# Four moves of work between engines in a one-core hybrid decoder layer

## The chip, the cores and the metric

The kernel runs on one core of one Trainium2 chip. The metric is the device time of one execution in microseconds (us), first instruction to last as the device reports it; lower is better. The engines are TensorE (PE in the rows; PEld is its weight load), VectorE (DVE), ScalarE (ACT), GpSimd (POOL) and SyncE (SP, which here issues nearly all the transfers). Each engine runs its own instructions strictly in the order in which they were written down for it.

## What is computed

One decoder layer for one sequence: SEQ = D_MODEL = 1024, all in float32. Cut to what matters here:

```python
mod = jnp.dot(jax.nn.silu(c), w_ada) + b_ada          # adaLN, 6 vectors of 1024
shift1, scale1, gate1, shift2, scale2, gate2 = split(mod, 6)
h = _rmsnorm(x, norm1_w) * (1.0 + scale1) + shift1
qa, ka, va, iq, ik, iw, qr, kr, vr, gr, ga, gb = split(jnp.dot(h, w_in))
# qa, ka, iq, ik, qr, kr are rotated by their positions
score = einsum('bqh,bqhs->bqs', iw, relu(einsum('bqhd,bsd->bqhs', iq, ik)))   # indexer
idx   = top_k(score, 256)                              # per query, causal
y_a   = attention(qa, ka, va, over idx only) @ w_attn_proj
ret   = retention(qr, kr, vr)                          # 4 heads, chunks of 128
y_r   = (silu(gr) * groupnorm_per_head(ret)) @ w_ret_proj
x = x + gate1 * ((sigmoid(ga) * y_a + sigmoid(gb) * y_r) @ w_out)
h2 = _rmsnorm(x, norm2_w) * (1.0 + scale2) + shift2
x = x + gate2 * ((silu(h2 @ w_gate) * (h2 @ w_up)) @ w_down)
return _rmsnorm(x, final_norm_w)
```

## The kernel before, in words

Every matrix product is done as three passes of 32-bit matmuls over a split of both factors in a high and a low part (`whi`, `wlo`, `hT_hi`, `hT_lo`). The high part is a copy on ACT, the low part a subtraction on POOL (L80, L756) or on DVE; the pairs live in a ring of 11. The weights come in by SP as blocks of 128x512 or 128x1024.

The order of the work on each engine is fixed ahead of time by a scheduler that goes through the program with priorities. `turns_after(a, b)` adds an order (no wait of its own): `a` is placed behind `b` in the list of instructions. Work whose priority is lowered by `LATE` fills places that the scheduler deems free. The stages, with the times at which the profiled execution is there:

- Startup, to about 100 us: the norm of x, the modulation vectors shift1 and scale1, and the first projections.
- V projection and indexer scores, about 100 to 230 us. `score_units` (L403) works out the score tiles; between them stand the first of 32 *modulation steps* of `mod_work` (L506). They are for the four vectors that are needed later: first m = 2 and 5 (the gates), then m = 3 and 4 (shift2, scale2). A step loads a block `mw` of 128x1024 of `w_ada` (two buffers) and adds it, times a column of silu(c), to `macc` on DVE (L525 for a vector's first step, L527 for the other seven). Behind the eighth step of a gate, `mod_gate` (L554) multiplies `macc` by a tile of ones on PE and adds the vector's bias, which `gateb` has from a broadcast load (one buffer, one load and one sum on L562 per half). Behind the eighth step of m = 3 and 4, `mod_cols` (L541) transposes `macc` (L547) and reduces it (L548, L550, L552). Each step is tied behind `summed[-1]`, the last score sum that was written down.
- The search, `select_all` (L449): the 256th largest score of each row is found by bisection, bit by bit. One pass is six counts `eq` (L463, tiles of 128x384 to 128x1024) and two small instructions (`rej` L468, `cand` L483), all on DVE; there are 31 passes and a last one. The passes have low priority, and some are tied to points of the program by the list `passes`.
- Retention, about 230 to 474 us: for two pairs of heads (`hp` = 0, 1) a *qk stage* (project, rotate, transpose) and a *V stage*. In the V stage each of eight tiles projects `vs`, makes two scores `inn` (`inner`: PE L674, DVE L676) and runs a chunk of the tile before for two heads (`chunk`: PE L684, L685, L689; DVE `rst` L693/L695; ACT `on` L698; DVE statistics L701 and L702, of which the last is kept in `chunked[0]`). In the V stage of `hp` = 0 two modulation steps are written down behind each tile.
- The gate stage, about 474 to 840 us: products with the weights of gr, q, k, gb and ga, in `Stream` objects that save one product in eight by sums of blocks (seven products `M1` to `M7` of 12 matmuls each). The results gather in `kept`, `sums` and `spare`, where `add` (L824, DVE) adds a product and `copy` (L821, ACT) starts one. `behind(i)` (L1029) runs behind product i: it ties search passes to `genv.added` and rotates the first channels of q and k, which earlier streams put in `rot_d`. `rope_load` fetches one half of the tokens, `rope_store` multiplies it by the tables (POOL L991, L992, L994, L995), adds (DVE L993, L996), splits (ACT L755, POOL L756) and stores.
- Attention, projections, FFN and the last norm, 840 us to the end.

## Time and profile before

| | |
|---|---|
| runs | 1747.34 us median of 3 (1744.49 to 1750.73) |
| profiled execution | 1744.53 us, its span 1742.7 us |
| mean granted TensorE clock | 0.995 |
| busy: PE, DVE, ACT, POOL | 97%, 71%, 43%, 49% of the span |

The profiled execution ran on one core and its trace holds every instruction with its start, its duration and, where its engine sat idle ahead of it, what released it. The span runs from the first instruction to the last; the execution's own time is 1.8 us longer. A share of busy time is a mean over stages that have different limits. What a change is worth is found where PE, the engine with 97%, sits idle: there a row says how long and which instruction ended it.

### The profile page before, as it was taken

What the parts mean: (1) busy time and instruction counts of PE and PEld (TensorE: products, weight loads), DVE (VectorE), ACT (ScalarE), POOL (GpSimd) and SP (SyncE); (2) the same over time, 40 slices, a digit from 0 to 9 for tenths busy, and PEclk for the clock granted to TensorE, in tenths of its full rate; (3) what the DMA queues carried; (4) which work ended last, traced back from release to release, by engine and by line L of the source; (5) the groups of instructions that cost most, each with busy time, mean ns of one, the idle gap of its engine ahead of it and who ended that gap; (6) DMA issues with size and microseconds to landing.
All of it is one profiled execution on the core that took longest, in us unless ns stands there. A gap on an engine that the chain in (4) does not pass through costs nothing.

```text
span 1742.7 us, 24594 instructions
## 1 busy us (share of the span) xinstructions
PE 1685.4 (97%) x8266; PEld 1391.7 (80%) x8266; DVE 1234.4 (71%) x2118; ACT 755.3 (43%) x1469; POOL 856.8 (49%) x855
## 2 busy tenths in 40 slices
PE   5899999999999999999999999999999999999998
PEld 4797777888887887888777888888888888878887
DVE  7528798898899577666576666885666555778664
ACT  3625542332454344530477235643333333445444
POOL 4563274583615578130346550055455554657573
PEclk9999999999999999999999999999999999999999
DMA  9535515412434356865761740044445444586652
GB/s 293 151 95 176 152 55 173 143 34 60 117 98 127 108 151 200 252 205 165 186 142 53 274 169 1 25 133 148 157 134 180 173 146 144 187 305 205 197 169 97
DMA packets 180063, 260.72 MB, mean 150 GB/s; under 512 B 13584, under 2 KB 111328, under 8 KB 177632
## 3 DMA queue, kind: packets, MB, share of 16 engines
q1 hardware_dynamic: 179936, 259.14, 47.6%
q8 instruction: 65, 1.06, 0.3%
q14 instruction: 62, 0.51, 0.1%
HBM read 192.51 MB, written 66.58 MB: 149 GB/s over the span
## 4 chain that ended last, share of the span: by engine, by line
PE 64%; DVE 3%; issue 1%; DMA 1%; POOL 1%; ACT 1%; SPq 0%; POOLq 0%; DVEq 0%; ACTq 0%
PE ya L843 4%; PE ya L841 4%; PE ya L845 4%; PE yb L843 3%; PE yb L841 3%; PE yb L845 3%; PE ya L1664 2%; PE ya L1663 2%; PE ya L1662 2%; PE pva L1183 2%; PE mm L841 2%; PE mm L843 2%; PE mm L845 2%; PE tra L1162 2%; PE lg L841 1%; PE lg L843 1%
## 5 line engine op out<-in xcount | busy, mean ns | idle before, releaser
L80 POOL TENSOR_TENSOR wlo<-wraw,whi 128x512 fp32r<-128x512 f32 (+2 forms) x116 | 147.9, 1285 | 136.6 <-ACT whi L77 100.1
L463 DVE TENSOR_SCALAR_CACHE_REDUCE eq<-score,cand 128x384 uint8<-128x384 f32 (+2 forms) x192 | 180.7, 941 | 4.0
L756 POOL TENSOR_TENSOR flo<-tmp,fhi 128x512 fp32r<-128x512 f32 x79 | 108.2, 1369 | 140.1 <-ACT fhi L755 100.5
L121 PE MATMUL mm<-whi,hT_hi 128*128 128x512 f32 (+1 forms) x432 | 162.0, 380 | 4.0 <-ACT qk L647 1.8
L123 PE MATMUL mm<-wlo,hT_hi 128*128 128x512 f32 (+1 forms) x432 | 161.6, 377 | 0.0
L124 PE MATMUL mm<-whi,hT_lo 128*128 128x512 f32 (+1 forms) x432 | 161.5, 376 | 0.0
L841 PE MATMUL ya<-hc,fhi 128*128 128x512 f32 x344 | 133.9, 390 | 2.0 <-DVE c L824 2.0
L843 PE MATMUL ya<-hc,fhi 128*128 128x512 f32 x344 | 134.1, 390 | 0.6 <-DVE hc L1302 0.6
L845 PE MATMUL ya<-hc,flo 128*128 128x512 f32 x344 | 133.1, 390 | 0.0
L1641 ACT ACTIVATE dslot<-draw 128x512 fp32r<-128x512 f32 x143 | 84.9, 627 | 93.1 <-DMA draw<-act_d 23.2
L756 POOL TENSOR_TENSOR flo<-raws,fhi 128x512 fp32r<-128x512 f32 x60 | 86.3, 1445 | 73.8 <-ACT fhi L755 42.4
L1642 DVE TENSOR_TENSOR dslot<-draw,dslot 128x512 fp32r<-128x512 f32 x81 | 86.4, 1098 | 50.7 <-ACT dslot L1641 49.3
L1642 POOL TENSOR_TENSOR dslot<-draw,dslot 128x512 fp32r<-128x512 f32 x62 | 95.5, 1554 | 53.0 <-ACT dslot L1641 51.0
L77 ACT ACTIVATE whi<-wraw 128x512 fp32r<-128x512 f32 (+2 forms) x116 | 67.2, 591 | 117.3 <-DMA wraw<-in_w_in_dram 56.6
L755 ACT ACTIVATE fhi<-tmp 128x512 fp32r<-128x512 f32 x82 | 51.5, 629 | 111.5 <-PE ya L843 57.2
L843 PE MATMUL yb<-hc,fhi 128*128 128x512 f32 x256 | 99.7, 390 | 0.0
L841 PE MATMUL yb<-hc,fhi 128*128 128x512 f32 x256 | 99.7, 389 | 0.0
L845 PE MATMUL yb<-hc,flo 128*128 128x512 f32 x256 | 99.5, 389 | 0.0
L121 PEld LDWEIGHTS mm<-whi,hT_hi 128*128 128x128 f32 x432 | 81.5, 190 | 16.1 <-ACT qk L647 2.2
L809 DVE TENSOR_TENSOR tmp<-raws 128x512 f32<-128x512 f32 x40 | 30.6, 768 | 86.7 <-POOL flo L756 86.7
L124 PEld LDWEIGHTS mm<-whi,hT_lo 128*128 128x128 f32 x432 | 81.7, 189 | 12.4
L1151 POOL TENSOR_SCALAR sx<-sx,mx 128x128 f32<-128x128 f32 (+7 forms) x64 | 47.4, 747 | 88.9 <-DVE mx L1150 66.3
(419 smaller groups left out, 4959.6 us busy)
## 6 DMA issues: line engine op xcount, KB each, us to landing
draw<-act_d SPq DMA_DIRECT2D x70, 256.0 KB
mw<-in_w_ada_dram SPq DMA_DIRECT2D x32, 512.0 KB
act_d<-c SPq DMA_DIRECT2D x58, 256.0 KB
raw<-in_w_in_dram SPq DMA_DIRECT2D x26, 512.0 KB
raws<-in_w_ffn_gate_dram SPq DMA_DIRECT2D x24, 512.0 KB
raws<-in_w_ffn_up_dram SPq DMA_DIRECT2D x24, 512.0 KB
dw<-in_w_ffn_down_dram SPq DMA_DIRECT2D x22, 512.0 KB
dw_d<-dw SPq DMA_DIRECT2D x10, 1024.0 KB
```

What stands on the lines that cost most here:

```text
L77: ins = nc.scalar.activation(hi[:, :n], raw[:, :n], AF.Copy)
L80: nc.gpsimd.tensor_sub(lo[:, :n], raw[:, :n], f32(hi[:, :n]))
L121: ins = nc.tensor.matmul(ps, lhsT=ahi, rhs=whi[:, :n], start=(i == 0), stop=False)
L123: nc.tensor.matmul(ps, lhsT=ahi, rhs=wlo[:, :n], start=False, stop=False)
L124: nc.tensor.matmul(ps, lhsT=alo, rhs=whi[:, :n], start=False, stop=(i == last))
L463: ins = [nc.vector.tensor_scalar(eq[:, :sc.shape[1]], sc, thr[j], None, op0=op, op1=ALU.add, accum_out=cnt[:, j:j + 1]) for j, sc in enume ...
L756: return ins, (eng or nc.gpsimd).tensor_sub(lo, src, f32(hi))
L841: mm = nc.tensor.matmul(ps, lhsT=whi[:, k, :], rhs=hhi[:, k, :], start=own and k == 0, stop=False, skip_group_check=True)
L843: nc.tensor.matmul(ps, lhsT=whi[:, k, :], rhs=hlo[:, k, :], start=False, stop=False, skip_group_check=True)
L845: nc.tensor.matmul(ps, lhsT=wlo[:, k, :], rhs=hhi[:, k, :], start=False, stop=k == 3, skip_group_check=True)
L1641: nc.scalar.activation(slot[:, 0], raw, AF.Copy)
L1642: lo_eng.tensor_sub(slot[:, 1], raw, f32(slot[:, 0]))
```

## The change

It has four parts.

1. The bias row of a gate comes by one load of 128x1024, written down at the fourth step of its vector, in place of two loads of 128x512 in `mod_gate`. The tile of ones moves into `spare`, to make room.
2. In the V stage of `hp` = 0 the modulation steps from the second tile on are tied behind the statistics of the tile (`chunked[0]`), where they were tied behind the last score sum.
3. The search passes that are tied to the gate stage's groups are each tied two groups later: pass 22 stands where pass 24 did, and so on.
4. `rope_store` becomes a generator of three steps, one step behind each of six products: the four multiplications on POOL, the sum and difference on DVE, and the split with its stores. The second half is loaded at M6 in place of M7.

```diff
@@ -500,7 +500,7 @@
-    ones = modp.tile([P, P], F32, name="ones")
+    ones = spare[:, :P]
     nc.vector.memset(ones, 1.0)
@@ -527,10 +527,12 @@
             if behind is not None:
                 turns_after(ins, behind)
+            if k == 3 and m in (2, 5):
+                bias = gate_bias(m)
             yield
             if k == KT - 1:
                 if m in (2, 5):
-                    mod_gate(m, m // 5, acc)
+                    mod_gate(m // 5, acc, bias)
@@ -551,12 +553,15 @@
-    def mod_gate(m, i, acc):
+    def gate_bias(m):
+        bias = modp.tile([P, D], F32, name="gateb", bufs=1)
+        nc.sync.dma_start(out=bias, in_=b_ada[m * D:(m + 1) * D].rearrange("(o d) -> o d", o=1).partition_broadcast(P))
+        return bias
+
+    def mod_gate(i, acc, bias):
         for hf in range(2):
             cs = slice(hf * H, (hf + 1) * H)
-            g = modp.tile([P, H], F32, name="gateb", bufs=1)
-            nc.sync.dma_start(out=g, in_=b_ada[m * D + hf * H:m * D + (hf + 1) * H]
-                              .rearrange("(o d) -> o d", o=1).partition_broadcast(P))
+            g = bias[:, cs]
             gp = ps_lg()
@@ -722,6 +727,8 @@
             if hp == 0:
+                if t:
+                    summed.append(chunked[0])
                 for _ in range(2):
                     next(mgen, None)
@@ -985,15 +992,18 @@
-    def rope_store(hf, r, tab):
+    def rope_turn(hf, r, tab):
+
         cs = slice(hf * H, (hf + 1) * H)
         t = [f32(x) for x in ring_pair()]
         nc.gpsimd.tensor_mul(t[0], r[0], tab[0])
         nc.gpsimd.tensor_mul(t[1], r[1], tab[1])
-        nc.vector.tensor_sub(t[0], t[0], t[1])
         nc.gpsimd.tensor_mul(r[0], r[0], tab[1])
         nc.gpsimd.tensor_mul(r[1], r[1], tab[0])
+        yield
+        nc.vector.tensor_sub(t[0], t[0], t[1])
         nc.vector.tensor_add(r[1], r[1], r[0])
+        yield
         for a, src in enumerate((t[0], r[1])):
@@ -1024,22 +1034,22 @@
-    rope, staged = {}, {}
+    rope, staged = [], {}
...
-        if i >= 15 and (i - 15) % 7 == 0 and 24 + (i - 15) // 7 < len(passes) - 1:
-            turns_after(passes[24 + (i - 15) // 7], genv.added)
+        if i >= 15 and (i - 15) % 7 == 0 and 22 + (i - 15) // 7 < len(passes) - 1:
+            turns_after(passes[22 + (i - 15) // 7], genv.added)
...
-            if n == 8 and m in ("M1", "M7"):
-                rope[len(rope)] = rope_load(len(rope))
-            if n == 9 and m in ("M5", "M2"):
-                rope_store(int(m == "M2"), *rope[int(m == "M2")])
+            if n == 8 and m in ("M1", "M6"):
+                rope.append(rope_turn(len(rope), *rope_load(len(rope))))
+            if n == 9 and m != "M4":
+                next(rope[int(m in ("M3", "M7", "M2"))], None)
```

How the instructions stand on an engine is listed below for three places, before and with the change (`out<-in` and the shape; line numbers are those of the kernel listed, so L676 before is L681 with the change). First DVE at the first score `inn` of the V stage of `hp` = 0. Before:

```order
L463 TENSOR_SCALAR eq,cnt<-score_769,cand 128x512
L463 TENSOR_SCALAR eq,cnt<-score_770,cand 128x640
L527 SCALAR_TENSOR_TENSOR macc<-mw,colT,macc 128x1024
L463 TENSOR_SCALAR eq,cnt<-score_771,cand 128x768
L527 SCALAR_TENSOR_TENSOR macc<-mw,colT,macc 128x1024
L676 TENSOR_TENSOR inn<-tr,rmask 128x128
L463 TENSOR_SCALAR eq,cnt<-score_772,cand 128x896
L527 SCALAR_TENSOR_TENSOR macc<-mw,colT,macc 128x1024
```

With the change:

```order
L463 TENSOR_SCALAR eq,cnt<-score_772,cand 128x896
L463 TENSOR_SCALAR eq,cnt<-score_773,cand 128x1024
L468 TENSOR_SCALAR rej<-cnt 128x6
L483 SCALAR_TENSOR_TENSOR cand<-cand,rej 128x6
L681 TENSOR_TENSOR inn<-tr,rmask 128x128 x3
L706 BN_STATS st_3216<-on 128x6
L698 COPY rst<-lg 128x256
L707 BN_AGGR mv<-st_3216 128x2
L681 TENSOR_TENSOR inn<-tr,rmask 128x128
```

Before, the eight steps of m = 3 stand among the counts here, six of them ahead of the first `inn` and two behind it; now none stands ahead of it. With the change the eight steps of m = 3 follow from the first chunk's statistics on, and the eight of m = 4 behind them, the last three behind the last chunk's statistics.

Second, DVE at the first `inn` of the V stage of `hp` = 1. Before:

```order
L463 TENSOR_SCALAR eq,cnt<-score_770,cand 128x640
L463 TENSOR_SCALAR eq,cnt<-score_771,cand 128x768
L463 TENSOR_SCALAR eq,cnt<-score_772,cand 128x896
L676 TENSOR_TENSOR inn<-tr,rmask 128x128
L463 TENSOR_SCALAR eq,cnt<-score_773,cand 128x1024
```

With the change:

```order
L463 TENSOR_SCALAR eq,cnt<-score_770,cand 128x640
L681 TENSOR_TENSOR inn<-tr,rmask 128x128
L463 TENSOR_SCALAR eq,cnt<-score_771,cand 128x768
L463 TENSOR_SCALAR eq,cnt<-score_772,cand 128x896
L463 TENSOR_SCALAR eq,cnt<-score_773,cand 128x1024
```

The `inn` stands two counts earlier in its pass. Third, POOL over the rotation of the second half of q and k (`wlo<-raw` and `wlo<-wraw` are low parts of weights, `wlo<-whi` and `wlo<-wlo,whi` those of the rotated rows). Before:

```order
L991 TENSOR_TENSOR whi<-whi 128x512
L756 TENSOR_TENSOR wlo<-raw_4945,whi 128x512
L756 TENSOR_TENSOR wlo<-wraw,whi 128x512
L756 TENSOR_TENSOR wlo<-raw_4946,whi 128x512
L756 TENSOR_TENSOR wlo<-wraw,whi 128x512
L992 TENSOR_TENSOR wlo<-wlo 128x512
L994 TENSOR_TENSOR whi<-whi,wlo 128x512
L995 TENSOR_TENSOR wlo<-wlo,whi 128x512
```

With the change:

```order
L999 TENSOR_TENSOR whi<-whi 128x512
L763 TENSOR_TENSOR wlo<-wlo,whi 128x512
L763 TENSOR_TENSOR wlo<-wraw,whi 128x512
L1000 TENSOR_TENSOR wlo<-wlo 128x512
L1001 TENSOR_TENSOR whi<-whi,wlo 128x512
L763 TENSOR_TENSOR wlo<-raw_4941,whi 128x512
L763 TENSOR_TENSOR wlo<-wraw,whi 128x512
L1002 TENSOR_TENSOR wlo<-wlo,whi 128x512
```

Four low parts of weights stood together within the four multiplications; now four low parts stand there two by two, one of them that of the first half's rotated rows.

## Rows read from the trace of the kernel before

**Rows 1.** The page: busy time, share of the span and instructions of each engine.
```profile
PE 1685.4 (97%) x8266; PEld 1391.7 (80%) x8266; DVE 1234.4 (71%) x2118; ACT 755.3 (43%) x1469; POOL 856.8 (49%) x855
```
**Rows 2.** Timeline of PE: start us, duration us, instruction, idle before it, releaser.
```profile
186.01 0.39 PE L424 MATMUL lg<-khi,qst 128*128 128x256 f32 x1 [1.82 <-DVE gateb L562]
...
290.85 0.80 PE L674 MATMUL tr<-qkT 128*128 128x128 f32 x2 [3.38 <-DVE inn L676]
...
413.51 0.71 PE L674 MATMUL tr<-qkT 128*128 128x128 f32 x4 [1.31 <-DVE inn L676]
...
536.54 0.50 PE L841 MATMUL mm<-hT_hi,whi 128*128 128x512 f32 x1 [2.01 <-DVE kept L824]
...
674.78 0.50 PE L841 MATMUL lg<-S,whi 128*128 128x512 f32 x1 [1.38 <-ACT kept L821]
...
694.14 0.50 PE L841 MATMUL lg<-hT_hi,whi 128*128 128x512 f32 x1 [2.12 <-ACT whi L755]
```
**Rows 3.** Windows: stretch, length, busy us by engine, PEclk, DMA share, GB/s.
```profile
0.00:40.00 40.00, 19.80 (x78) 15.38 (x79) 29.19 (x57) 14.10 (x24) 16.26 (x21) 0.96 1.00 285
...
286.00:296.00 10.00, 6.62 (x25) 5.16 (x24) 8.99 (x15) 0.38 (x1) 0.00 (x0) 0.83 0.72 216
296.00:345.00 49.00, 48.97 (x235) 41.32 (x234) 37.27 (x96) 18.38 (x36) 24.94 (x43) 1.00 0.42 132
345.00:411.00 66.00, 65.87 (x310) 54.04 (x309) 61.53 (x129) 23.57 (x59) 51.95 (x78) 1.00 0.21 57
480.00:536.00 56.00, 54.24 (x238) 44.27 (x237) 55.90 (x93) 29.10 (x52) 14.76 (x10) 1.00 0.33 100
640.00:670.00 30.00, 30.00 (x134) 24.82 (x134) 20.07 (x29) 14.84 (x25) 27.91 (x20) 1.00 0.64 203
```
**Rows 4.** Timelines of SP and DVE around the first gate bias.
```profile
182.00 0.33 SPq L558 DMA_DIRECT2D gateb<-in_b_ada_dram  x1
...
185.27 0.69 DVE L562 TENSOR_TENSOR gateb<-gateb,lg 128x512 f32<-128x512 f32 x1 [3.40 <-DMA gateb<-in_b_ada_dram]
```
**Rows 5.** Timeline of DVE ahead of the first `inn` of hp = 0.
```profile
272.06 2.98 DVE L525 TENSOR_SCALAR macc<-mw,colT 128x1024 f32<-128x1024 f32 x1
...
289.31 1.28 DVE L527 SCALAR_TENSOR_TENSOR macc<-mw,colT,macc 128x1024 f32<-128x1024 f32 x1 [0.52 <-DMA mw<-in_w_ada_dram]
290.51 0.28 DVE L676 TENSOR_TENSOR inn<-tr,rmask 128x128 f32<-128x128 f32 x1
```
**Rows 6.** Line view of L527 in 300 to 420 us: ns min/median/max, first and last start.
```profile
L527 DVE SCALAR_TENSOR_TENSOR macc<-mw,colT,macc x7: 1275/1317/2123, 326.4 to 348.1; 128x1024 f32<-128x1024 f32 x7
```
**Rows 7.** Timeline of DVE: last reductions of hp = 0, counts ahead of hp = 1.
```profile
353.53 1.26 DVE L548 TENSOR_REDUCE modr<-tr 128x4 f32<-128x512 f32 x2
...
411.04 1.01 DVE L463 TENSOR_SCALAR_CACHE_REDUCE eq<-score,cand 128x768 uint8<-128x768 f32 x1
...
412.10 1.15 DVE L463 TENSOR_SCALAR_CACHE_REDUCE eq<-score,cand 128x896 uint8<-128x896 f32 x1
...
413.17 0.29 DVE L676 TENSOR_TENSOR inn<-tr,rmask 128x128 f32<-128x128 f32 x1
```
**Rows 8.** The page: groups of instructions, busy, mean ns; then DVE's timeline.
```profile
L463 DVE TENSOR_SCALAR_CACHE_REDUCE eq<-score,cand 128x384 uint8<-128x384 f32 (+2 forms) x192 | 180.7, 941 | 4.0
...
535.81 1.28 DVE L824 TENSOR_TENSOR kept<-kept,mm 128x512 f32<-128x512 f32 x2
```
**Rows 9.** Timelines of DVE, ACT and POOL at the rotation of q and k.
```profile
672.89 0.69 DVE L993 TENSOR_TENSOR whi<-whi,wlo 128x512 f32<-128x512 f32 x1
...
673.61 0.63 ACT L755 ACTIVATE whi<-whi 128x512 fp32r<-128x512 f32 x1 [2.78 <-DVE whi L993]
...
687.80 1.74 POOL L995 TENSOR_TENSOR wlo<-wlo,whi 128x512 f32<-128x512 f32 x1
...
689.58 1.77 DVE L996 TENSOR_TENSOR wlo<-wlo,whi 128x512 f32<-128x512 f32 x1
...
691.38 0.63 ACT L755 ACTIVATE whi<-wlo 128x512 fp32r<-128x512 f32 x1 [1.73 <-DVE wlo L996]
```

## The prediction

> **What bounds the kernel now.** I read the busy shares first, then PE's idle time with what ended it, then the windows around each of those places, and last the timeline of the engine that ended the wait. TensorE is busy for 97% of the span, VectorE for 71% [rows 1], so only what shortens an idle stretch of PE counts. Six stretches of PE's timeline lie where the change works [rows 2]: 1.82 us ended by a gate bias sum, 3.38 and 1.31 us ended by the first scores `inn` of the two V stages, 2.01 us ended by a sum into `kept`, and 1.38 and 2.12 us ended by ACT during the rotation of q and k. They add up to 12.0 us. The other idle time of PE lies in the startup or in stages that the diff does not touch. One of the six costs more than it shows: in the ten microseconds around the 3.38 us, the granted clock is 0.83 where it is 1.00 elsewhere [rows 3]. That is 10 x 0.17 = 1.7 us of full-speed time, spent at the lower of the two levels (1.2 in place of 2.4 GHz) right behind the idle stretch. So the six are worth 13.7 us at most.
>
> **Part 1, the bias row.** The load of `gateb` is issued at 182.00 us, and DVE idles 3.40 us until it lands and the sum can run at 185.27 [rows 4]; PE waits behind that sum. With the change the whole row is loaded four steps earlier, and the second half has no load of its own to wait for. The 1.82 us go; I take 1.8. What is late next is the score work itself, at which PE waits nowhere near. The first bias row has room from the start of the kernel on, so its load is written down among the startup's, and it is twice as long: 256 KB more at 285 GB/s are 0.9 us in a stretch in which the DMA share is 1.00 [rows 3]. PE is busy for only 19.8 of those 40 us, and waits for VectorE more than for data; the instructions there change places too. Bounds: 2.5 us to either side (a gain, if the places change for the better; beyond the 0.9 us, if several loads fall behind). I take a loss of 0.5, about half the load.
>
> **Part 2, modulation steps in the first V stage.** Before the first `inn` at 290.51 stand the steps of m = 3: one took 2.98 us, another 1.28 after a wait of 0.52 us for its weights [rows 5]. Six steps stand ahead of `inn`, 2.98 + 5 x 1.28 = 9.4 us; even at 1.28 for the first they are 7.7. All of these leave, and both figures exceed the 3.38 us that PE waits, so the wait goes, and with it the clock's fall: 3.4 + 1.7 = 5.1 us gained. The path that then sets the moment is PE itself.
>
> The steps are paid for later. In the stretch 296 to 345 us, VectorE is busy 37.27 of 49 us [rows 3]; eight more steps of 1.28 us are 10.2, which makes 47.5 of 49. That is fuller than 345 to 411 (61.53 of 66), where PE loses 0.13 us, and not as full as 480 to 536 (55.90 of 56), where PE loses 1.8 us of 56 [rows 3]. Bounds for the V stage: 0, and 4.9 us if all eight steps take the 2.12 us of the slowest one there in place of 1.32 [rows 6] (8 x 0.8 = 6.4, less the 1.5 us still free). I take 1.5, by the fullest row: 1.8 x 49 / 56.
>
> The first `inn` of the second V stage is the next to be late. Behind the last chunk's statistics three steps (3 x 1.28 = 3.8 us) and the reductions (1.26 us for the pair [rows 7], and two small sums that I estimate at 0.2 each) come in front of the free search passes, in which VectorE has no rest up to that `inn`. In return the `inn` stands two counts earlier (1.01 + 1.15 = 2.2 us [rows 7]). PE itself comes there 1.8 us later: between the last chunk and the blocked score stand four more matmuls, at 0.22 us each (134 in 30.00 us [rows 3]), and eight transposes, which I count at half of that. So 3.8 + 1.6 - 2.2 - 1.8 = 1.4 us more to wait, 1.31 becoming 2.7. Bounds: 0, if VectorE gains elsewhere in the stretch, and 3.1 if the clock falls too (1.4 + 1.7). I take 1.4: the wait that the clock followed was longer, 3.38 us.
>
> **Part 3, the search passes.** PE waits 2.01 us at 536.54 until the sum into `kept` at 535.81 [rows 2, 8], with VectorE busy 55.90 of the 56 us before it. Tying the passes two groups later takes one pass out of the way of that sum: six counts of 0.94 us on average [rows 8] and two small instructions, 6 us or more. The wait is a third of that, so it goes: 2.0 us gained. The pass comes later in the gate stage, whose 640 to 670 window has VectorE at 20.07 of 30 [rows 3]. If that cover were gone, the final selection would end later by one pass, 6 us, and the attention behind it with it.
>
> **Part 4, the rotation.** PE's 1.38 us are ended by ACT's copy into `kept`, which stands behind the split of the rotated rows at 673.61, released by VectorE's difference at 672.89 [rows 2, 9]. With the change this difference stands one count earlier and the split ahead of other copies. PE's 2.12 us are ended by the fourth weight split behind ACT's `whi<-wlo` at 691.38; that waits for VectorE's 689.58, which takes 1.77, and this for POOL's fourth multiplication at 687.80 [rows 9]. The multiplications are no shorter afterwards, and POOL is full (27.91 of 30 us before it [rows 3]); four low parts still lie among them. The second half is loaded one product earlier. Bounds: 0 (POOL sets the end as before) and 3.5 (both waits go). I take 2.3, two thirds: the first wait wholly, of the second less than half.
>
> **The sum.** Gains 1.8 + 5.1 + 2.0 + 2.3 = 11.2; losses 0.5 + 1.5 + 1.4 = 3.4; net 7.8 us. Against the profiled execution of 1744.5 that is 1736.7. The profiled execution is 2.8 us below the median of the runs shown, near the fastest; a median is forecast, so I take 7.8 from 1747.3: **1739.5 us**. A measurement of this kernel can tell about 0.3% (5.2 us) from no change.
>
> **A rule weighed.** A step has two inputs in SBUF (`mw` and `macc`), and the stretch of the V stage holds 24.94 us of POOL work [rows 3]; the row shows that the steps there mostly keep their time: 1.32 us in the median, 2.12 at most [rows 6]. The Trainium skill (SBUF — State Buffer, Who interferes with whom) says that a VectorE instruction with two SBUF inputs contends with a GpSimd instruction that reads SBUF, and that the later of the two is blocked for the whole of the other. If that held for every moved step, each would be longer by up to a low part's time; the sum would come out by the last rival below. The row speaks for some steps blocked and most not.
>
> **The rivals.**
>
> *VectorE becomes the bound in the first V stage, and PE is throttled at the second.* For it: 47.5 of 49 us leaves nothing for a slow step, and the passes are tied there too. Against it: PE has up to six scores `inn` in hand, and 345 to 411 ran nearly as full at no loss. V stage 4.9 in place of 1.5, second `inn` 3.1 in place of 1.4: net gain 7.8 - 3.4 - 1.7 = 2.7, so 1744.6.
>
> *More goes than I count.* Both waits of the rotation vanish (3.5), VectorE keeps pace in the V stage and ahead of the second `inn` (0 and 0), and the startup is unchanged: 1.8 + 5.1 + 2.0 + 3.5 = 12.4, so 1734.9; with 2.5 from the startup 1732.4. For it: every wait is shorter than the work taken from in front of it. Against it: VectorE's work only moves.
>
> *Parts 3 and 4 do not do what they say.* The sum into `kept` waits for another product's work, and POOL's chain sets the rotation's end as before. Then 7.8 - 2.0 - 2.3 = 3.5 are left: 1743.8. For it: POOL at 27.91 of 30. Against: a pass is three times the wait.
>
> *Slower: POOL blocks the moved steps.* All sixteen steps now lie in the V stage beside POOL's low parts. At 2.4 us each (between the slowest L527 there, 2.12, and the 2.98 of the L525 [rows 5, 6]) they are 16 x 1.08 = 17.3 us longer, with next to no free time on VectorE, and PE waits at each `inn`. The net is 7.8 + 1.5 - 17.3 = -8.0: 1755.3. It decides from 9.3 / 16 = 0.6 us per step on, a mean of 1.9 us; slower by over 0.3% from 0.9 us on. Against it: the median of 1.32.
>
> **How the numbers follow.** The forecast 0.50 (its own range 1735 to 1744), VectorE the bound 0.17, more than counted 0.15, parts 3 and 4 idle 0.10, slower 0.08. Below 1742.1 (faster by over 0.3%): most of the forecast (0.45), all of the second, a part of the others (0.06): 0.66. Above 1752.6: 0.07. The rest is 0.27. The range leaves out the far end of the slow case and of the good one: 1731 to 1748.
>
> **What would show it.** Right: no wait of PE at the gate bias, none at the first `inn` of the first V stage with a granted clock of 1.00 there, 2 to 3 us at the first `inn` of the second, none at `kept` near 530, and one wait of about 1.2 us at the rotation. Wrong: PE waiting several times for `inn` or `rst` between 300 and 350, with L527 above 1.9 us in the mean; a startup that ends some us later than before; a new wait in the gate stage behind the pass that came later, above all at the end of the search.

## The result, and the profile after

The changed kernel takes 1738.01 us, the median of 7 runs (1733.46 to 1741.31), against 1747.34 us before, now the median of 7 runs. The ratio is 0.9935, with a 95% interval of 0.9912 to 0.9959. Here and below the ratio is formed from the undisturbed runs of one session, so it need not be the quotient of the two medians. The forecast was 1739.5 us, in a range of 1731 to 1748: the time lies 1.5 us below the forecast, and the kernel is faster.

The profiled execution took 1733.46 us (its span 1731.7 us, the mean granted clock 0.995 as before). It is the fastest of the seven, 11.1 us below the profiled execution of before, while the medians lie 9.3 us apart. What this extra is made of is told with the last experiment.

The busy shares of the page:

```profile
PE 1683.4 (97%) x8266; PEld 1391.3 (80%) x8266; DVE 1234.5 (71%) x2118; ACT 753.5 (44%) x1469; POOL 862.7 (50%) x855
```

PE's busy time is 2.0 us less than before [rows 1], with the same number of instructions. The clock does not explain this: a stretch at half clock has gone in the retention (1.7 us), but the startup has more of it than before (below). The other 9 us of the span are idle time. PE's timeline shows the waits that are left where the change works, with the idle time and its releaser in brackets, and ahead of them one at 141 that the profile of before does not have:

```profile
141.16 0.44 PE L424 MATMUL lg<-khi,qst 128*128 128x384 f32 x1 [0.94 <-ACT rl L428]
231.45 0.51 PE L121 MATMUL mm<-whi,hT_hi 128*128 128x512 f32 x1 [1.78 <-ACT qk L652]
410.38 0.71 PE L679 MATMUL tr<-qkT 128*128 128x128 f32 x4 [0.28 <-DVE inn L681]
452.15 0.67 PE L689 MATMUL lg<-rst,qkT 128*128 128x256 f32 x2 [0.62 <-DVE rst L700]
516.70 0.50 PE L850 MATMUL mm<-hT_lo,whi 128*128 128x512 f32 x1 [1.03 <-DVE hT_lo L641]
663.35 0.50 PE L848 MATMUL mm<-S,whi 128*128 128x512 f32 x1 [1.51 <-ACT kept L828]
700.34 0.50 PE L848 MATMUL mm<-hT_hi,whi 128*128 128x512 f32 x1 [0.35 <-DVE sums L831]
```

Of the six waits of [rows 2], that at the gate bias and that at the first `inn` of the first V stage have no row any more. The one at the second V stage is 0.28 us in place of 1.31. The sum into `kept` has gone, but 1.03 us behind a low part `hT_lo` on DVE stand nearby. Of the rotation's 1.38 and 2.12 us, 1.51 are left, with 0.35 behind a sum. The row at 231.45 is not the change's: before has the same wait, and in the window 229 to 239 both kernels have a granted clock of 0.83.

The windows of the changed kernel (columns as in [rows 3]: busy time of PE, PEld, DVE, ACT, POOL, granted clock, DMA share, GB/s):

```profile
229.00:239.00 10.00, 8.22 (x29) 6.28 (x29) 9.33 (x19) 4.56 (x15) 7.45 (x9) 0.83 0.18 54
283.00:293.00 10.00, 10.00 (x50) 8.44 (x49) 1.67 (x7) 1.78 (x5) 1.00 (x3) 1.00 0.05 15
293.00:342.00 49.00, 49.00 (x236) 41.66 (x235) 42.24 (x99) 18.56 (x40) 30.92 (x44) 1.00 0.61 186
342.00:408.00 66.00, 66.00 (x313) 54.54 (x312) 60.42 (x121) 21.56 (x53) 50.52 (x74) 1.00 0.25 68
```

The stretch 283 to 293 answers to the one of before whose clock was 0.83: it is at 1.00 now, and VectorE, which PE waited for there, is busy for only 1.67 of 10 us. The V stage behind it (293 to 342) has 42.24 us of VectorE work, where the prediction counted 47.5, and PE is never idle in it.

### The profile page after: what moved, and what is told of

It reads as the page before. It is cut to its first block, busy times and chain, and to the rows that moved or that the text cites. A ratio compares the mean times of both kernels' runs of the same rounds, so it can differ in the third digit from the quotient of the medians.

```text
span 1731.7 us, 24591 instructions
## 1 busy us (share of the span) xinstructions
PE 1683.4 (97%) x8266; PEld 1391.3 (80%) x8266; DVE 1234.5 (71%) x2118; ACT 753.5 (44%) x1469; POOL 862.7 (50%) x855
## 4 chain that ended last, share of the span: by engine, by line
PE 76%; DVE 10%; DMA 4%; issue 3%; POOL 3%; ACT 2%; SPq 1%; POOLq 0%; DVEq 0%; ACTq 0%
PE ya L850 4%; PE ya L848 4%; PE ya L852 4%; PE yb L850 3%; PE yb L848 3%; PE yb L852 3%; DVE eq L463 3%; PE ya L1674 2%; PE ya L1672 2%; PE ya L1673 2%; PE mm L121 2%; PE mm L124 2%; PE mm L123 2%; PE pva L1193 2%; PE mm L850 2%
## 5 line engine op out<-in xcount | busy, mean ns | idle before, releaser
L1161 POOL TENSOR_SCALAR sx<-sx,mx 128x128 f32<-128x128 f32 (+7 forms) x64 | 47.5, 747 | 88.2 <-DVE mx L1160 64.7
```

## The experiments

### Each part alone

Before ran beside these four at a median of 1749.0 us (1743.16 to 1757.69). The first took part 1 alone (the diff of `mod_work` and `mod_gate` and the tile of ones; nothing else).

```diff
-    ones = modp.tile([P, P], F32, name="ones")
+    ones = spare[:, :P]
...
+            if k == 3 and m in (2, 5):
+                bias = gate_bias(m)
```

> The kernel before with part 1 alone (whole bias row loaded early, ones in the spare tile). Theory, the parts add up: the wait of 1.82 us at the gate bias sum is gone, the five other waits of the list stand within 0.3 us of before (3.38 with the granted clock at half behind it, 1.31, 2.01, 1.38, 2.12), and the time is 2 us below before. Rival, the startup pays it back (twice the bias row, other places of the startup's instructions): PE's idle time in the first 100 us is 2 us or more above before's 27 us and the time is that of before.

Measured: 1755.14 us (1748.83 to 1759.63), ratio 1.0019 (1.0000 to 1.0037). So part 1 alone gains nothing, and is likelier a loss. The wait at the gate bias had gone and the startup was no longer than before; neither theory says where the time went. PE's timeline and then DVE's do:

```profile
283.16 0.33 PE L668 MATMUL tr<-ident,rq 128*128 128x128 f32 x1 [3.44 <-POOL rq L665]
294.53 0.49 PE L679 MATMUL tr<-qkT 128*128 128x128 f32 x2 [3.31 <-DVE inn L681]
423.11 0.80 PE L679 MATMUL tr<-qkT 128*128 128x128 f32 x2 [7.48 <-DVE inn L681]
...
266.96 7.22 DVE L468 TENSOR_SCALAR rej<-cnt 128x6 int32<-128x6 f32 x1
274.22 0.17 DVE L483 SCALAR_TENSOR_TENSOR cand<-cand,rej 128x6 int32<-128x6 int32 x1
396.54 8.81 DVE L468 TENSOR_SCALAR rej<-cnt 128x6 int32<-128x6 f32 x1
```

Three waits of 14.2 us together, each followed by half clock, and two instructions `rej` of 7.22 and 8.81 us. `rej` is the search's small instruction between two passes, on a tile of 128x6; the like-sized `cand` behind it takes 0.17 us. In the profile of before the longest `rej` took 1.26 us. POOL's timeline of the same kernel shows what the first one waited for:

```profile
266.86 1.33 POOL L80 TENSOR_TENSOR wlo<-wraw,whi 128x512 fp32r<-128x512 f32 x1
268.12 0.49 POOL L665 TENSOR_TENSOR rq<-rra,rrb 128x128 f32<-128x128 f32 x1
...
273.38 0.78 POOL L661 TENSOR_TENSOR rrb<-qk,sinr 128x256 f32<-128x256 f32 x1
```

`rej` starts at 266.96, behind the start of a low part on POOL (266.86), and ends at 274.18; POOL works without a gap until 274.16, through eight instructions. The second `rej` ends at 405.35, and POOL's other unbroken run at 405.32. So a held `rej` lasts until POOL's run ends, and everything behind it on DVE is that much later. This became the theory of the experiments behind these four, and it is not in the prediction.

Part 2 alone, a single line of order:

```diff
             if hp == 0:
+                if t:
+                    summed.append(chunked[0])
```

> The kernel before with part 2 alone (modulation steps behind each tile's statistics). Theory: the 3.38 us ahead of the first score and the half clock behind it go, 5 us; the gate bias wait (1.82) and the rotation's (1.38 and 2.12) stay. At the first score of the second V stage the theory of the prediction wants 2.7 us; the theory read from the trace of the changed kernel (there the last statistics came 2 us behind the last chunk where they came 6 us behind it before, since ACT's copy was no longer late) wants 0.5 us at most. Rival for part 3's gain: if the wait of 2.01 us near 535 us goes here too, it was VectorE's lead out of the retention that removed it, and not the passes tied later; the theory wants it to stay at 1.5 or more.

Measured: 1739.19 us (1738.36 to 1744.19), ratio 0.9942 (0.9921 to 0.9962). PE's timeline has no wait ahead of either first `inn`, and the clock there is 1.00. At the other places of the change its waits are these, and the rotation's 0.24 and 2.18 us:

```profile
187.25 0.39 PE L424 MATMUL lg<-khi,qst 128*128 128x256 f32 x1 [0.58 <-DVE gateb L562]
519.46 0.50 PE L845 MATMUL mm<-hT_lo,whi 128*128 128x512 f32 x1 [1.97 <-DVE hT_lo L636]
522.20 0.50 PE L845 MATMUL mm<-hT_lo,whi 128*128 128x512 f32 x1 [0.86 <-DVE hT_lo L636]
```

One line carries nearly the whole gain. The wait at `kept` is gone here without part 3, as the rival had it, and waits for `hT_lo` stand in its place. Two waits that were to stay did not: the gate bias has 0.58 us in place of 1.82, and the first of the rotation 0.24 in place of 1.38.

Part 3 alone:

```diff
-        if i >= 15 and (i - 15) % 7 == 0 and 24 + (i - 15) // 7 < len(passes) - 1:
-            turns_after(passes[24 + (i - 15) // 7], genv.added)
+        if i >= 15 and (i - 15) % 7 == 0 and 22 + (i - 15) // 7 < len(passes) - 1:
+            turns_after(passes[22 + (i - 15) // 7], genv.added)
```

> The kernel before with part 3 alone (passes tied two groups later). Theory: the wait of 2.01 us at the sum into kept falls to 1.1 or less, and nothing else of the list changes by over 0.3 us; the time is 1 to 2 us below before. Rival, VectorE comes late out of the retention and the wait stays at 2 us without part 2: then the time is that of before.

Measured: 1745.85 us (1739.51 to 1751.45), ratio 0.9981 (0.9963 to 0.9999). In place of the 2.01 us at `kept` PE has the second of these waits alone; the first stands ahead of the first `inn`, where before has 3.38 us:

```profile
288.27 0.49 PE L674 MATMUL tr<-qkT 128*128 128x128 f32 x2 [1.86 <-DVE inn L676]
...
518.88 0.50 PE L843 MATMUL mm<-hT_lo,whi 128*128 128x512 f32 x1 [0.88 <-DVE hT_lo L636]
```

So part 3 gains about 1.1 us at that place, and what is late next is the low part of the activations, which shares DVE with the passes. That nothing else would change by over 0.3 us did not hold: besides the 1.86 us, behind which the clock stays at 1.00, the gate bias has 0.94 us in place of 1.82. Both places lie ahead of the gate stage, where part 3 ties its passes, and why they differ was not followed up.

Part 4 alone, `rope_turn` in three steps with the load at M6 (the end of its diff):

```diff
...
-            if n == 9 and m in ("M5", "M2"):
-                rope_store(int(m == "M2"), *rope[int(m == "M2")])
+            if n == 9 and m != "M4":
+                next(rope[int(m in ("M3", "M7", "M2"))], None)
```

> The kernel before with part 4 alone (rotation in three steps). Theory: the two waits of 1.38 and 2.12 us add up to 2.0 or less, the other four stay, and the time is 1.5 to 2 us below before. Rival, POOL's four multiplications among the low parts set the end and the gain in the changed kernel came from VectorE, which has another part of the search there: the two waits add up to 3 us or more.

Measured: 1744.57 us (1742.05 to 1752.32), ratio 0.9976 (0.9958 to 0.9995). The waits at both `inn` and `kept` are there as before (3.05, 1.34 and 2.02 us), that at the gate bias is 0.72 us in place of 1.82; of the rotation's two, one of 1.51 us is left, as the theory has it.

### The held instruction

The three parts without the line of part 2:

```diff
-                if t:
-                    summed.append(chunked[0])
```

> The changed kernel without part 2 (parts 1, 3 and 4). Theory, the parts hang together: the bias row moved early makes VectorE late in the retention unless the modulation steps leave it, so the waits of PE between 270 and 430 us add up to 8 us or more as with part 1 alone (14.2), and the time is at or above that of before, 1747 to 1753. Rival, the parts add up (from the waits each removes: 1.8 for the bias row, 2.0 and 2.3 for the others): 1741 to 1743, with 5 us or less of waits in that stretch.

Measured: 1752.09 us (1742.17 to 1754.08) beside 1746.6 (1741.48 to 1752.65), ratio 1.0014 (0.9993 to 1.0035). Parts 1, 3 and 4 together gain nothing that can be measured. The ten runs fall in two groups, four of 1742 to 1745 us and six of 1752 to 1754. The profiled execution belongs to the slower; its waits between 270 and 430 us add up to 12.2 us (1.80, 2.94 and 7.46), as the theory has it, and its DVE and PE timelines show the held `rej` again:

```profile
267.71 7.23 DVE L468 TENSOR_SCALAR rej<-cnt 128x6 int32<-128x6 f32 x1
396.92 8.78 DVE L468 TENSOR_SCALAR rej<-cnt 128x6 int32<-128x6 f32 x1
...
423.46 0.79 PE L679 MATMUL tr<-qkT 128*128 128x128 f32 x2 [7.46 <-DVE inn L681]
```

Next the form of the instruction was tried. `rej` was written as one with two inputs, the second a column of powers of two in the unused tile `rank`, first in the kernel with part 1 alone, then in the whole change:

```diff
+        pw = rank[:, 0:64].bitcast(F32)
+        for bit in range(31):
+            nc.gpsimd.memset(pw[:, bit:bit + 1], float(1 << bit))
...
-            rejected(1 << bit)
+            nc.vector.scalar_tensor_tensor(rej, cnt, float(TOPK), pw[:, bit:bit + 1].to_broadcast([P, n]),
+                                           op0=ALU.is_lt, op1=ALU.mult)
```

> Part 1 alone, with the search's small instruction rej (one input from SBUF and two constants) written with a second input from SBUF, a tile of powers of two, in place of one constant; the values are the same. Theory: with part 1 alone rej took 7.22 and 8.81 us at 267.0 and 396.5, each time until the end of an unbroken run of POOL, and that made VectorE late; with two inputs it waits for one POOL instruction at most, as cand does (1.3 us at most). Then no rej is above 1.5 us, the waits of PE between 270 and 430 us fall from 14.2 to 6 us or less, and the time is 1749 or less. Rival, the order of the instructions and the stores on SP ahead of the weight loads made it late, and rej only filled the time: rej is short, but the waits stay at 10 us or more and the time at 1753 or more.

> The changed kernel with the same other form of rej. Theory: its longest rej, 3.36 us at 391.5, goes to 1.3 or less, the wait of 0.28 us at the first score of the second V stage goes, and the time is 0 to 3 us below the changed kernel's. Rival: two inputs cost more on the whole, since every rej then waits for a POOL instruction, where now most take 0.17 us: the mean of rej rises above 0.55 us and the time by 1 us or more.

Measured: with part 1 alone 1748.96 us (1748.14 to 1759.58), ratio 1.0024 (1.0004 to 1.0045); with the whole change 1737.67 us (1737.31 to 1739.71), ratio 0.9943 (0.9923 to 0.9964). DVE's timelines, of the kernel with part 1 and then of the whole change with this `rej`:

```profile
266.03 7.22 DVE L484 SCALAR_TENSOR_TENSOR rej<-cnt,rank 128x6 int32<-128x6 f32 x1
395.97 8.78 DVE L484 SCALAR_TENSOR_TENSOR rej<-cnt,rank 128x6 int32<-128x6 f32 x1
```

```profile
267.11 7.20 DVE L484 SCALAR_TENSOR_TENSOR rej<-cnt,rank 128x6 int32<-128x6 f32 x1
394.45 5.87 DVE L484 SCALAR_TENSOR_TENSOR rej<-cnt,rank 128x6 int32<-128x6 f32 x1
```

The form makes no difference; the theory that two inputs wait for one POOL instruction only fell. The second kernel showed something else: with the steps moved, 13.1 us of held VectorE work cost PE 4.67 us at `rq` (285.62) with the half clock behind it, and 0.32 us at the first `inn` of the second V stage, where the kernels with held `rej` and without part 2 lose over 7.

The wait of 1.78 us at 231 was tried next: ACT writes the projections `qk` into one of two buffers there, and the next ones wait. The first two tiles were put into buffers that are free then:

```diff
+        qk0 = [big_tile(3 - t, [P, 4, 2, HD], F32, "qk0") for t in range(2)] if hp == 0 else []
...
-            qk = retp.tile([P, 4, 2, HD], F32, name="qk", bufs=2)
+            qk = qk0[t] if t < len(qk0) else retp.tile([P, 4, 2, HD], F32, name="qk", bufs=2)
...
```

> The changed kernel with the projected q, k of the first two tiles of the first qk stage in buffers that are free before the indexer's are. Theory: the wait of 1.78 us at 231.45, where ACT copies them only behind the last score pieces, goes, and with it the half clock behind it (1.7 us): 2 to 3.5 us below the changed kernel. Rival: the copies stand behind the score pieces on ACT anyway and the wait stays within 0.5 us.

Measured: 1746.0 us (1738.76 to 1749.05), ratio 0.9980 (0.9963 to 0.9996). The edit did what it says: PE is busy for 10.00 of the ten microseconds from 229, at a clock of 1.00. Still the kernel is slower than the whole change without it. DVE's and PE's timelines:

```profile
266.89 6.63 DVE L468 TENSOR_SCALAR rej<-cnt 128x6 int32<-128x6 f32 x1
394.27 10.62 DVE L468 TENSOR_SCALAR rej<-cnt 128x6 int32<-128x6 f32 x1
...
426.76 0.80 PE L682 MATMUL tr<-qkT 128*128 128x128 f32 x2 [6.56 <-DVE inn L684]
```

POOL's unbroken run is sixteen instructions long at the second hold and ends at 404.86. Beside the 6.56 us PE waits 2.38 us for `macc` at 368.65, and the last statistics of the first V stage end 7.3 us behind PE's last chunk there (361.34 and 354.07), where they end 1.9 us behind it in the change. Why the edit does this was not followed up.

### Part 1 left out

Since part 1 alone was no gain, two versions were run without it: the change less part 1 (its diff is that of the first experiment, taken back), and the same with the early `qk`. Before ran beside them at 1746.72 us (1742.37 to 1755.26).

> The changed kernel without part 1 (parts 2, 3 and 4). Theory, part 1 gives its 1.8 us in the score stage but makes VectorE's rej run into POOL's unbroken runs more often, about even on the whole: 1736 to 1740, a wait of 0.5 to 1.8 us at the gate bias, no rej above 1.5 us. Rival, part 1 is needed for its gain: 1740 to 1743, with the wait at the gate bias at 1.8 us and all others as in the changed kernel.

> The same, with the projected q, k of the first two tiles in buffers that are free earlier. With part 1 this removed the wait of 1.78 us near 231 and the half clock behind it, but in the profiled execution rej took 6.63 and 10.62 us at 266.9 and 394.3 and PE lost 6.56 us at the first score of the second V stage. Theory, those long rej belong to kernels with part 1: here no rej is above 1.5 us and the time is 2 to 3.5 us below the kernel without part 1. Rival, they come from POOL starting its rotation earlier: a rej above 5 us again, a wait of 4 us or more near 420, and a time of 1742 or more.

Measured: 1738.21 us (1733.21 to 1740.97), ratio 0.9938 (0.9913 to 0.9962), and 1748.8 us (1746.81 to 1754.32), ratio 1.0008 (0.9991 to 1.0024). The first is level with the whole change; the second loses it all: its trace has `rej` of 6.62 and 10.16 us, and PE waits 3.03 and 6.57 us at the first `inn` of the two V stages. The timelines of the first, PE, DVE, PE:

```profile
185.33 0.38 PE L424 MATMUL lg<-khi,qst 128*128 128x256 f32 x1 [1.35 <-DVE gateb L562]
...
391.49 6.41 DVE L468 TENSOR_SCALAR rej<-cnt 128x6 int32<-128x6 f32 x1
...
413.42 0.80 PE L674 MATMUL tr<-qkT 128*128 128x128 f32 x2 [4.65 <-DVE inn L676]
```

The gate bias wait is back, and held `rej` stand in two kernels without part 1: the theory that part 1 brings the held instruction fell as well. No version beat the change.

### The same kernels again

Two kernels were profiled a second time, unchanged: the three parts without part 2, and the whole change.

> The changed kernel without part 2 once more, unchanged, for a second execution: its ten times fell into two groups, four from 1742 to 1745 and six from 1752 to 1754. Theory, the groups are executions without and with a rej that waits for the end of an unbroken run of POOL: at 1742 to 1746 there is none above 1.5 us and the wait near 416 is 2 us or less; at 1751 or more there are one or two of 5 us or more, and the wait near 416 is about 7.5 us. Rival: the long rej is there at either time, and something else divides the groups.

> The changed kernel once more, unchanged, for a second execution: the profiled one, 1733.5, is the fastest of its seven, and the median is 4.6 us longer. Theory, what the median has and the profiled execution has not is a rej that waits for the end of an unbroken run of POOL: at 1736 or more there is one of 5 us or more (near 267 or 394), and PE's waits near 281 (for POOL's rq) or 410 (for the first score) add up to 2 us or more, where the profiled execution has 0.3. Rival, the 4.6 us are spread over the startup and the transfers: no rej above 3.5 us, the two waits below 1 us, and the difference is found before 230 us or after 840 us.

Measured, one execution each: 1751.99 us, again of the slower group, with `rej` of 7.21 and 8.79 us and PE's wait of 7.45 us; and 1738.83 us, which is 5.4 us above the profiled execution of the same program. Its theory held: a `rej` of 7.20 us, and waits of 2.92 and 0.29 us. These two executions of one program show what a held `rej` does by itself. Timelines of DVE, SP, ACT and POOL, first the execution of 1733.46 us, then that of 1738.83 us, whose last row is PE's:

```profile
266.51 1.25 DVE L468 TENSOR_SCALAR rej<-cnt 128x6 int32<-128x6 f32 x1
269.64 0.69 DVE L567 TENSOR_TENSOR gateb<-gateb,lg 128x512 f32<-128x512 f32 x1
270.74 0.42 SPq L98 DMA_DIRECT2D wraw<-in_w_in_dram  x1
273.43 0.63 ACT L77 ACTIVATE whi<-wraw 128x512 fp32r<-128x512 f32 x1 [4.25 <-DMA wraw<-in_w_in_dram]
278.66 0.47 POOL L665 TENSOR_TENSOR rq<-rra,rrb 128x128 f32<-128x128 f32 x1
```

```profile
266.76 7.20 DVE L468 TENSOR_SCALAR rej<-cnt 128x6 int32<-128x6 f32 x1
275.64 0.69 DVE L567 TENSOR_TENSOR gateb<-gateb,lg 128x512 f32<-128x512 f32 x1
276.74 0.42 SPq L98 DMA_DIRECT2D wraw<-in_w_in_dram  x1
279.39 0.63 ACT L77 ACTIVATE whi<-wraw 128x512 fp32r<-128x512 f32 x1 [10.11 <-DMA wraw<-in_w_in_dram]
284.69 0.45 POOL L665 TENSOR_TENSOR rq<-rra,rrb 128x128 f32<-128x128 f32 x1
285.20 0.33 PE L668 MATMUL tr<-ident,rq 128*128 128x128 f32 x1 [2.92 <-POOL rq L665]
```

(Later in the qk stages both executions also have a `rej` of 3.36 us.) Read downwards, each row is 6.0 us later in the second execution, from the second row on. The gate sum (L567) stands behind `rej` on DVE; SP's store of `gate_d` waits for that sum; the load of the next weight block stands behind the store on SP; ACT's split waits for the load, POOL's low part for the split, and POOL's `rq` stands behind the low part. PE waits 2.92 us for it and then runs ten microseconds at a granted clock of 0.83, 1.7 us more. These 4.6 us are most of the 5.4 between the two executions. Most of the rest is the rotation, which waits 2.63 us here where it waited 1.51 and 0.35.

## Why the prediction was right

**The forecast.** 7.8 us were predicted, 9.3 measured between the medians. Term by term, from the profiled executions, which lie 11.1 us apart. The stretches are measured by the times at which PE starts the same matmul before and after; a row's gain is what the difference of the two times grew by since the row above:

| stretch or term | predicted | measured | from |
|---|---|---|---|
| startup | -0.5 | -0.1 | 105.22 before, 105.37 after |
| scores ahead of the gate bias | none | -1.3 | 177.16 and 178.61; 0.94 us of wait at 141.16 |
| gate bias | +1.8 | +2.1 | 217.69 and 217.03 |
| retention: first V stage's `inn` and clock | +5.1 | +5.1 | 3.38 us gone, clock 1.00 for 0.83 |
| retention: V stage | -1.5 | 0 | PE 49.00 of 49 us |
| retention: second V stage's first `inn` | -1.4 | +1.0 | 1.31 for 0.28 |
| retention in all (with the three above) | +2.2 | +7.0 | 485.95 and 478.34 |
| `kept` | +2.0 | +1.6 | 567.73 and 558.55 |
| rotation | +2.3 | +1.9 | 776.83 and 765.70 |
| the rest | none | -0.1 | spans 1742.7 and 1731.7 |

The stretches add up to 11.1 us; of the retention's 7.0, the three terms are 6.1 and 0.9 were not placed. In the startup the clock falls for longer (0.96 and 0.97 over 0 to 40 and 40 to 100 us become 1.00 and 0.91), but PE is idle for 1.0 us less of the first 100, and the same matmul starts 0.1 us later. The mechanism of the largest term was right. That the forecast lies within 1.5 us of the median is in part luck. The retention gave 4.8 us more than forecast, and the score stage, which is in no term, cost 1.3; its wait at 141 is not in the second execution of the same program. The two profiled executions of the changed kernel differ by 5.4 us, most of it through the held `rej`, which the prediction does not have.

**The step that was wrong in sign: the first `inn` of the second V stage.** The prediction had VectorE later there by 3.8 + 1.6 - 2.2 = 3.2 us against PE's 1.8. Both deltas were nearly so: from the last chunk to the blocked score PE takes 62.1 us in place of 60.5, and VectorE, from the end of the last statistics to `inn`, 60.1 in place of 55.5 (4.6 more, of which 2.0 are the steps' wait for their weights). What the sum had left out is where VectorE's stretch begins. The last statistics, before and then after, in DVE's timelines:

```profile
357.28 0.43 DVE L701 BATCH_NORM_STATS2 st<-on 128x6 f32<-128x256 f32 x1 [2.07 <-ACT on L698]
```

```profile
349.54 0.43 DVE L706 BATCH_NORM_STATS2 st<-on 128x6 f32<-128x256 f32 x1 [0.52 <-ACT on L703]
```

Measured from the start of PE's last chunk (351.75 and 348.04), the end of these statistics comes 6.0 us behind it before and 1.9 us behind it after. These four microseconds more than pay for the steps. A difference between two engines was summed from one common moment, and the two did not share that moment. This is the account of the whole change only. In part 2 alone the statistics end 5.3 us behind the chunk (ACT's copy stands there behind a product that waits 3.33 us for POOL), yet no wait is left: VectorE's stretch is 1.2 us longer than before there and not 4.6, since `rej` takes 2.3 us of it where it takes 5.9 with the whole change, and the steps wait 0.2 us for their weights where they wait 2.0. The expectation of that run had the right number by another way.

**The loss in the V stage: a size that was off.** 1.5 us were taken, 0 measured. Part of that is a count: eight more steps were put into the stretch, and three of the same steps were priced again behind the last chunk. The stretch from 293 us holds 11 steps (13.4 us) where the one from 296 us held 7 (8.8 us), so VectorE has 42.24 us of work and not 47.5. VectorE starts the stage with time in hand, as its timeline shows at the scores, where it now waits for PE:

```profile
287.33 0.29 DVE L681 TENSOR_TENSOR inn<-tr,rmask 128x128 f32<-128x128 f32 x1 [4.59 <-PE tr L679]
```

And the moved steps keep their time. The group of L527 from 283 to 360 us (least, median and longest duration in ns):

```profile
L527 DVE SCALAR_TENSOR_TENSOR macc<-mw,colT,macc x14: 1252/1278/1515, 294.9 to 356.8; 128x1024 f32<-128x1024 f32 x14
```

1.28 us in the median and 1.52 at most, where the slower rival needed a mean of 1.9. The rows of POOL say much of why: of the sixteen steps only two start while it works at a low part (at 327.45 and 334.39, 1.00 and 1.51 us), where before five did, of 1.32 to 2.12 us. That so few would meet is not in the prediction. The rival was right that POOL can hold VectorE, and wrong about where: not at the steps of the V stage but at `rej` in the two stages ahead, where POOL works without a gap.

**`kept` and the rotation.** The sum into `kept` no longer holds PE, and what was late next, which the prediction did not name, are low parts `hT_lo` on DVE at 517 (1.03 us). In the rotation the shares came out the other way round. The prediction took the first wait as gone wholly and the second as less than half gone; the second has gone, with 0.35 us behind a sum near it, and the first is still there with 1.51 us at 663.35. ACT's copy into `kept` still stands behind a split that waits for VectorE's difference. DVE's and ACT's timelines:

```profile
660.91 0.69 DVE L1004 TENSOR_TENSOR whi<-whi,wlo 128x512 f32<-128x512 f32 x1
661.70 0.63 ACT L762 ACTIVATE whi<-whi 128x512 fp32r<-128x512 f32 x1 [1.76 <-DVE whi L1004]
```

POOL's two products for it end at 655.91, but on DVE the difference stands behind three counts. The forecast's 2.3 allowed for 1.2 us left; 1.9 were, by two errors of opposite sign.

**The parts do not add up.** The prediction added them. By the medians' ratios part 2 alone gives 0.9942 and all four 0.9935, while the other three without it give 1.0014. Part 1 is worth nothing measurable (0.9938 without it). Its wait does go, but it was 0.58, 0.72, 0.94, 1.35, 1.70 and 1.82 us in six executions of kernels that lack part 1. Between the profiled executions part 2 alone gains 5.8 us (1744.53 and 1738.72), near its 5.1; between the medians it is more. What it does beyond its 5.1 us is in part open. At the first `inn` no kernel with part 2 and the old `qk` buffers waits, behind a held `rej` or not. At the second, the slack comes with the early statistics, and these are not part 2's alone: they end 1.7 to 2.5 us behind PE's last chunk in the change and with the other `rej`, and 5.3 us behind it in the two kernels with part 2, the old `qk` buffers and no part 1. So a `rej` of 5.87 us cost 0.32 us there in the one, and one of 6.41 us cost 4.65 us in the other. That the wide spread of the kernel before (1741 to 1758 us over all its runs) is held instructions too is likely but not shown: its one profile has no `rej` above 1.26 us. It has a held step, though. The 2.98 us of L525 [rows 5], which the prediction took as the step's cost, start within an unbroken run of POOL that ends at 274.49, 0.55 us ahead of the step's end; with the change the two L525 take 0.72 and 1.00 us.

**A rule weighed, once more.** The rows above show a 128x6 instruction on VectorE held for 7.22 us through eight POOL instructions. The Trainium skill (SBUF — State Buffer, Who interferes with whom) says of a VectorE instruction in a two-port mode beside one of GpSimd: "Whoever issues first gets the shared pair for the whole instruction; the other **fully blocks**", and counts `tensor_scalar` among the operations that can enter such a mode. The trace agrees that VectorE is blocked, by how the ends coincide: all eighteen `rej` above 3 us in the fourteen traces end 0.02 to 0.03 us behind an end of POOL's, and POOL's next instruction starts only afterwards. It differs in the length, which in these is that of the rest of POOL's run and not of one instruction (1.3 us at most there). The measurement decides.

**Still open.** Why `rej` is held for one POOL instruction in some executions and for the whole run in others of the same program: in both it starts within 0.1 us of the start of a low part on POOL (266.51 and 266.44 in the execution of 1733.46 us, 266.76 and 266.70 in that of 1738.83, where POOL's run then ends at 273.94 and `rej` at 273.96). The faster group of the kernel without part 2 was never caught by a profile. Not tried: a gap in POOL's runs, and the store of `gate_d` on another queue than SP.

## What to carry to other kernels

A wait of PE that costs its clock as well, and that VectorE work with a later due time causes, is worth removing first: here one line of order gave nearly all of the gain. When two engines are compared over a stretch, take both from the same moment, and look up what starts each of them. When parts are priced one by one, run the set without the largest: parts that each remove a wait can be worth nothing while a longer one stands behind them.

## What the runs showed of the hardware

- A VectorE instruction of 0.17 us on a 128x6 tile can take 7.20, 8.81 or 10.62 us while GpSimd runs instruction after instruction. All eighteen above 3 us ended where GpSimd's unbroken run did, with one input or two.
- This differs between executions of one program: 1.25 and 7.20 us for the same instruction, 1733.46 and 1738.83 us for the kernel. A single profile can therefore show a kernel with or without it.
- SP's queue passes such a delay on: a store that waits for VectorE moved the loads of weights behind it by 6.0 us.
- The granted clock fell to 0.83 over ten microseconds around or behind waits of PE of 1.78, 2.92 and 3.38 us. It stayed at 1.00 over 229 to 239 us with the same wait (1.79 us) in part 1 alone, and around 1.86 us in part 3 alone. So the prediction's argument that a shorter wait would spare the clock is not borne out by these lengths.
